# RWKV time mixing: where the value projections run, and where they are kept until the chains use them

## The chip, the cores and the metric

The kernel runs on one core of a Trainium2 chip. The metric is the device time of one execution in microseconds. The program has one launch, on fixed inputs, and is compiled once; a planner in the compiler puts the instructions of each engine in order.

## The reference, cut to what matters

Two layers of an encoder trunk over 256 tokens of width 2048. Each layer is a mixer and a squared-ReLU MLP, both with a norm whose shift, scale and gate come from a conditioning vector. The mixer of the second layer is a bidirectional RWKV-7 with 32 heads of 64:

```python
xr, xw, xk, xv, xa, xg = [h + xx * mu[j] for j in range(6)]
r = heads(xr @ w_r); k = heads(xk @ w_k); v = heads(xv @ w_v)
g = jax.nn.sigmoid(xg @ g1) @ g2
...
sa = jnp.einsum('bhvk,bhk->bhv', state, -kk_t)
state = state * w_t[:, :, None, :] + sa[..., None] * (kk_t * a_t)[:, :, None, :] + v_t[..., None] * k_t[:, :, None, :]
o_t = jnp.einsum('bhvk,bhk->bhv', state, r_t)
...
o = groupnorm(state_out) * gn_g + gn_b
y = ((o + bonus) * g) @ w_o
x = x + gate * y
```

The scan runs once forwards and once backwards. The three projections and the output are products of 256 x 2048 by 2048 x 2048 in float32. The `gate` of the residual is a third of the conditioning's product `silu(c) @ ada_w + ada_b`.

## The kernel before, in words

**Products.** A float32 product is made of three matmuls in a rounded format (lines 510, 511, 512, `prod`): high by high, high by low, low by high. The weights arrive in tiles of 128 x 1024 (512 KB), are cast on ScalarE (line 465) and the rest is taken on VectorE (line 466). A projection is cut in four blocks of 512 columns, one for each four pairs of heads. `stream` (line 999) yields a step for each of 16 row tiles; `rwkv_linear` (line 1025) issues 4 x 3 matmuls of 256 columns in each step. One weight tile and one input tile of 512 KB each serve two steps. `PF` = 3 weight tiles are asked for ahead. They lie in a pool `wp` of six buffers.

**Inputs.** `spill_mixes` (line 1282) makes the token-shifted inputs, split in high and low. The keys' input stays in SBUF (two tiles of 128 x 8 x 2 x 256, `self.xd[2]`); those of the receptances and the values are written to DRAM (`mix0`, `mix3`) and read back once for each block (line 1009).

**The keys stage** (n = 0 to 3). `mains` is a chain of generators: keys and receptances of blocks 0 to 3, then the values of block 0; `in_turn` starts the next one six steps (`LD`) before the last ends. Beside them run two lanes of `rwkv_keys` (line 1339), which make decay, keys and their triangular products for four pairs of heads and write them to DRAM, and `invert` (line 1417), 31 steps of two VectorE operations for a block's triangular inverse. `weave` (line 950) takes a step from the stream that is furthest behind by its weight.

**The chains** (p = 0 to 17). In round p run: the last six steps of chain p - 1 and the first seven of chain p (`pair_chain`, line 1543), with a priority of 1000 (`HA`, `HB`); the preparation of pair p + 1 (`pair_prep`, line 1472; before the rounds that of pair 0); the tail of pair p - 2 (`pair_tail`, line 1622); `MT` steps of `work()`, with `main` as its name; the inverse of block 3 in rounds 0 to 2, then `BG` halves of conditioning in rounds 3 to 14. `pair_load` (line 1445) asks for the data of pair p + 2. `work()` is the values of blocks 1 to 3, and then the output projection `rwkv_out` (line 1052): columns 2 and 3 over eight row tiles, whose sums are put aside in DRAM, then columns 0 and 1, then the rest. A unit of `rwkv_out` waits until the tails have made its row tiles (`ready`, line 1085). Round 17 takes what is left of `main`; after it come the last row tiles and the residual.

**Values.** Those of a block are a tile of 128 x 4 x 256 in SBUF, of pool `vp` or `p2`; `pair_prep` transposes a quarter of it (lines 1487 to 1489), and the tail multiplies it with the bonus (line 1630).

**Conditioning.** `bg` (line 331) keeps `AP` = 5 loads of 512 KB ahead in `wp` and does one half product on VectorE (line 362). 35 halves are left for this layer: 32 for its gate, 3 for the last MLP.

**Order.** The planner goes by priority, which is the order in which the code emits, raised for the chains, and by when inputs are ready. All loads named here are issued by SP, in one queue. `paced` (line 964) ties each step of `main` behind a matmul of the chains. The pools of the keys stage (`ws`, `xt`, `xk`, `rk`, `p1`) are closed before those of the chains (`p2`) open, which take their place in SBUF tile by tile. `pt` (line 944) takes PSUM from two pools of four banks in turn (`PQ`), or from one alone once `npt` is None, which `rwkv_out` sets when it begins.

Of the kernel before, what the change touches and what calls it, by code (L numbers as in the profile page):

```python
# [9 lines left out]
F32 = mybir.dt.float32  # L10
# [22 lines left out]
BG, IV, CH, MT, B0, B1, M0, M1, LD = (10, 10, 10, 10, 10, 10, 10, 10, 10, 5, 5, 5, 5, 5, 5, 5, 5, 5), 12, 7, (5, 5, 5, 5, 5, 5, 5, 5, 5, 5, 5, 2, 3, 2, 3, 2, 3, 2), 3, 14, 6, 6, 6  # L33
PK, PF = 8, 3
# [179 lines left out]
class Build:  # L214
# [21 lines left out]
    def run(self):  # L236
# [4 lines left out]
        self.cut, self.casts, self.wq = None, [], None  # L241
# [222 lines left out]
    def split(self, a, hi, lo, eng=None):  # L464
        c = self.nc.scalar.copy(hi, a)  # L465
        d = (eng or self.nc.vector).tensor_tensor(lo, a, hi, ALU.subtract)  # L466
        if eng is None:
            self.cut = d.ins
            self.casts = [c.ins]
# [18 lines left out]
    def load(self, name, n, i, pools):  # L488

        self.turn += 1  # L490
        w = self.t(pools[self.turn % len(pools)], [P, 2, NB], "w")
        src = self.A[name][n, i // 2][:, i % 2 * 2 : i % 2 * 2 + 2]
        if self.wq is None:
            self.dma = self.nc.sync.dma_start(w, src).ins
        else:
            with self.tc.issue_after(self.casts[-1]):
                self.wq.dma_start(w, src)
        self.tick(self.rate / 2)
        return w
# [499 lines left out]
    def stream(self, name, n, src, tiles):  # L999
# [4 lines left out]
        def ahead(i):  # L1004
            if isinstance(src, list):
                x = src[i // 4][:, 2 * i % 8 : 2 * i % 8 + 2]
            else:
                x = self.t(self.xt, [P, 2, 2, T], "x", bufs=self.xb, dt=F32R)
                nc.sync.dma_start(x.bitcast(F32), src[:, 2 * i : 2 * i + 2])
# [94 lines left out]
    def rwkv(self):  # L1104
# [7 lines left out]
        self.nd = [tc.dram_tile([P, 2, 1024], F32, name=f"nd{b}") for b in range(4)]  # L1112
        self.rx = [tc.dram_tile([4, 32, 1024], F32, name=f"rx{b}") for b in range(4)]
# [3 lines left out]
        with ExitStack() as st:  # L1117
# [5 lines left out]
            vp = self.pool(st, "vp", reuse_waits="tile")  # L1123
            vt = {}

            def values(n, pool):
                def tiles():
                    vt[n] = self.t(pool, [P, 4, T], "v")
                    return vt[n]

                yield from self.rwkv_linear("rw_v", n, 3, tiles)

# [3 lines left out]
            self.xd[2] = [self.t(xk, [P, 8, 2, T], f"xk{i}", dt=F32R) for i in range(2)]  # L1136
# [17 lines left out]
            mains = self.in_turn(mains + [values(0, vp)], LD)  # L1154
            with ExitStack() as st2:
# [12 lines left out]
                self.rate, self.wq = 0.0, None  # L1168
# [6 lines left out]
            with st1:  # L1175
                p1 = self.pool(st1, "p1", reuse_waits="tile")
                for n in range(4):
# [17 lines left out]
                    self.weave((self.take(mains, 34), 34 if n < 3 else 17), (lane(0), 21), (late(), 24), (self.invert(n - 1) if 0 < n <= IB else None, 34))  # L1195
            with ExitStack() as st1:
# [28 lines left out]
                def spread_gate(pool):  # L1225
                    r, g = self.need("tm", 2), self.t(pool, [P, 4, T], "v")
# [7 lines left out]
                self.weave((self.pair_prep(p2, Z[0], vt[0][:, 0, :]), 12), (self.take(main, M1), M1))  # L1234
                chains, self.gates = {}, []
                for p in range(18):
# [3 lines left out]
                    if p < 15:  # L1240
                        nx = self.pair_prep(p2, Z[p + 1], vt[(p + 1) // 4][:, (p + 1) % 4, :])
                    if p == 17:
                        self.npt = None
                        spread_gate(vp)
# [33 lines left out]
        self.wq = None  # L1278
# [3 lines left out]
    def spill_mixes(self, h, xx):  # L1282
        for j in (2, 0, 3):
            for k in range(0, KT, 2):
# [3 lines left out]
                if j == 2:  # L1288
                    x = self.xd[2][k // 8][:, k % 8 : k % 8 + 2]
# [182 lines left out]
    def pair_prep(self, rp, z, v):  # L1472
# [6 lines left out]
        z["v"] = v  # L1479
# [246 lines left out]
```

## Time and profile before

| | |
|---|---|
| runs | 3045.83, 3052.12, 3054.84 us (median 3052.12) |
| profiled execution | 3047.34 us; its span 3045.3 us |
| mean granted clock of TensorE | 0.973 |
| TensorE busy | 2871.4 us, 94% |
| VectorE, ScalarE, GpSimd busy | 2122.1, 1301.6, 522.2 us |
| HBM read, written | 706.08, 42.80 MB |

The span is the time from the first to the last instruction. A stretch is given by its start and end in microseconds from the start of the span. Busy time of TensorE is a union of its matmuls, so work at half clock counts as busy too; beside it stands the clock that was granted, as a share of 2.4 GHz. An "x" stands before a count of instructions. A float32 matmul outside of `prod` is two recorded matmuls. Some records are missing.

### The profile page before, as it was taken

The page shows a single profiled execution, that of the slowest core. Times are in us where ns is not written, and L with a number is a line of the kernel's source. Part 1 is how long each engine was busy: PE and PEld are TensorE (multiplying, and loading weights), DVE is VectorE, ACT ScalarE, POOL GpSimd, SP SyncE. Part 2 cuts the span into 40 slices and gives each one's busy share as a digit, 9 for nine tenths or more (in the row PEclk, how much of TensorE's full clock was granted, in tenths as well). Part 3 has the DMA queues.
Part 4 walks back from the last instruction along what each step waited for, and adds up shares of the span by engine and source line. Part 5 has one row for each costly group of instructions (what it writes and reads, how often), then busy time and mean ns, then how long its engine had stood idle before and what let it go on. Part 6 is the DMA issues. An engine that isn't in the chain of part 4 may idle for free. (4 is left out here: it accounts for less than half of the span.)

```text
span 3045.3 us, 52042 instructions
## 1 busy us (share of the span) xinstructions
PE 2871.4 (94%) x20308; PEld 2488.7 (82%) x20308; DVE 2122.1 (70%) x3126; ACT 1301.6 (43%) x1947; POOL 522.2 (17%) x574
## 2 busy tenths in 40 slices
PE   6999989999999999997999878999998999999998
PEld 2678776789988999886888777777778998899986
DVE  7899866657777788787768875775646776455454
ACT  3233334444443444443466542334445443344443
POOL 1211200011100011004354541322322110001000
PEclk9999999999999999998999987999999999999999
DMA  9978777747898988984987788997545777555552
GB/s 328 326 271 284 243 262 263 247 154 244 287 308 306 304 290 290 313 297 158 323 264 249 266 258 226 301 300 208 149 149 194 245 252 272 193 186 183 202 193 93
DMA packets 279970, 752.30 MB, mean 247 GB/s; under 512 B 73081, under 2 KB 99577, under 8 KB 278572
## 3 DMA queue, kind: packets, MB, share of 16 engines
q1 hardware_dynamic: 279148, 745.38, 73.1%
q8 instruction: 159, 2.61, 0.3%
q10 hardware_dynamic: 576, 3.60, 0.3%
q14 instruction: 87, 0.71, 0.1%
HBM read 706.08 MB, written 42.80 MB: 246 GB/s over the span
## 5 line engine op out<-in xcount | busy, mean ns | idle before, releaser
L466 DVE TENSOR_TENSOR f_wl<-f_w,f_wh 128x1024 fp32r<-128x1024 f32 x512 | 630.8, 1233 | 444.3 <-ACT f_wh L465 433.4
L465 ACT CAST f_wh<-f_w 128x1024 fp32r<-128x1024 f32 x512 | 538.0, 1052 | 748.4 <-PE f_mm L512 315.8
L511 PE MATMUL f_mm<-f_h,f_wh 128*128 128x256 f32 x2048 | 579.5, 283 | 0.0
L510 PE MATMUL f_mm<-f_h,f_wh 128*128 128x256 f32 x2048 | 579.5, 283 | 0.0
L512 PE MATMUL f_mm<-f_h,f_wl 128*128 128x256 f32 x2048 | 579.1, 283 | 0.0
L511 PE MATMUL f_mm<-f_wl,f_hid 128*128 128x512 f32 x1024 | 398.6, 389 | 1.1 <-DVE f_wl L466 1.1
L512 PE MATMUL f_mm<-f_wh,f_hid 128*128 128x512 f32 x1024 | 398.5, 389 | 0.0
L511 PEld LDWEIGHTS f_mm<-f_h,f_wh 128*128 128x128 f32 x2048 | 393.2, 192 | 0.1
L510 PEld LDWEIGHTS f_mm<-f_h,f_wh 128*128 128x128 f32 x2048 | 393.0, 192 | 0.1
L512 PEld LDWEIGHTS f_mm<-f_h,f_wl 128*128 128x128 f32 x2048 | 392.9, 192 | 0.0
L510 PE MATMUL f_mm<-f_wh,f_hid 128*128 128x512 f32 x1024 | 357.9, 389 | 0.0
L362 DVE SCALAR_TENSOR_TENSOR mix_w<-mix_w,mix_s 128x1024 f32<-128x1024 f32 x175 | 219.8, 1265 | 77.0 <-DMA mix_w<-in_ada_f 52.5
L466 POOL TENSOR_TENSOR f_hid<-f_u,f_hid 128x512 fp32r<-128x512 f32 x64 | 98.0, 1531 | 990.6 <-ACT f_hid L465 988.2
L362 DVE SCALAR_TENSOR_TENSOR f_w<-f_w,mix_s 128x1024 f32<-128x1024 f32 x174 | 233.6, 1345 | 2.6 <-DMA f_w<-in_ada_f 2.6
L511 PEld LDWEIGHTS f_mm<-f_wl,f_hid 128*128 128x128 f32 x1024 | 192.2, 188 | 41.3 <-DVE f_wl L466 1.7
L512 PEld LDWEIGHTS f_mm<-f_wh,f_hid 128*128 128x128 f32 x1024 | 192.3, 188 | 39.8
L510 PEld LDWEIGHTS f_mm<-f_wh,f_hid 128*128 128x128 f32 x1024 | 192.2, 188 | 39.7
L466 DVE TENSOR_TENSOR tm_wl<-tm_w,tm_wh 128x1024 fp32r<-128x1024 f32 x128 | 164.4, 1287 | 85.8 <-ACT tm_wh L465 81.6
L465 ACT CAST mix_wh<-mix_w 128x1024 fp32r<-128x1024 f32 x114 | 119.4, 1050 | 201.2 <-PE mix_mm L512 86.3
L510 PE MATMUL tm_mm<-tm_x,tm_wh 128*128 128x256 f32 x512 | 161.2, 316 | 12.3 <-DMA tm_x<-mix 10.8
L465 ACT CAST tm_wh<-tm_w 128x1024 fp32r<-128x1024 f32 x128 | 133.4, 1046 | 86.7 <-PE tm_mm L511 60.3
L466 DVE TENSOR_TENSOR mix_wl<-mix_w,mix_wh 128x1024 fp32r<-128x1024 f32 x114 | 142.4, 1254 | 38.8 <-ACT mix_wh L465 38.7
(456 smaller groups left out, 5494.6 us busy)
## 6 DMA issues: line engine op xcount, KB each, us to landing
f_w<-in_w SPq DMA_DIRECT2D x512, 512.0 KB, 5.1
f_w<-in_ada_f SPq DMA_DIRECT2D x125, 512.0 KB, 5.6
mix_w<-in_ada_mix SPq DMA_DIRECT2D x96, 512.0 KB, 6.2
mix_w<-in_w_in SPq DMA_DIRECT2D x80, 512.0 KB, 5.0
mix_w<-in_ada_f SPq DMA_DIRECT2D x64, 512.0 KB, 5.2
tm_x<-mix SPq DMA_DIRECT2D x64, 512.0 KB, 5.8
f_w<-in_ada_tm SPq DMA_DIRECT2D x49, 512.0 KB, 5.8
mix_w<-in_w_out SPq DMA_DIRECT2D x32, 512.0 KB, 4.6
```

The source lines that it names most:

```text
L362: V.scalar_tensor_tensor(w, w, 1.0, self.s[:, j * (D // 2) : (j + 1) * (D // 2)], ALU.mult, ALU.mult, accum_out=a[:, j, i : i + 1])
L465: c = self.nc.scalar.copy(hi, a)
L466: d = (eng or self.nc.vector).tensor_tensor(lo, a, hi, ALU.subtract)
L510: mm(out, lhsT=l[0], rhs=r[0], start=start, stop=False)
L511: mm(out, lhsT=l[0], rhs=r[1], start=False, stop=False)
L512: mm(out, lhsT=l[1], rhs=r[0], start=False, stop=stop)
```

## The change

The values of all four blocks are projected at the end of `mains`, in the weave of block n = 3 of the keys stage, which now takes 17 x 4 + 1 = 69 steps with a weight of `VL` = 34, where before it took 17 with a weight of 17. When the values' first generator starts, it takes eight tiles in place of the keys' input (which is now eight tiles instead of two) and loads the values' input into them once; all four blocks read it there. The values of a block go to a tile "gate" in `rk` and from there to DRAM (`vd`). `pair_load` reads 128 x 256 of them for each pair, before its other loads, into a tile "v" with six buffers, and `pair_prep` takes them from there. `work()` now begins with the output projection. `MT` is 4 in all rounds (before: 5 in rounds 0 to 10, then 2 and 3 in turn), `BG` is 3 (before: 10 in rounds 0 to 8, then 5). The gate's tile of line 1226 comes from `p2`. The second queue for weights (`wq`, `casts`), which was never set, is gone.

```diff
-BG, IV, CH, MT, ... = (10, 10, 10, 10, 10, 10, 10, 10, 10, 5, 5, ...), 12, 7, (5, 5, 5, 5, 5, 5, 5, 5, 5, 5, 5, 2, 3, 2, 3, 2, 3, 2), ...
+BG, IV, CH, MT, B0, B1, M0, M1, LD = 3, 12, 7, 4, 3, 14, 6, 6, 6
-PK, PF = 8, 3
+PK, PF, VL, NV = 8, 3, 34, 4
...
     def stream(self, name, n, src, tiles):
...
             if isinstance(src, list):
-                x = src[i // 4][:, 2 * i % 8 : 2 * i % 8 + 2]
+                x = src[i]
...
     def rwkv(self):
...
+        self.vd = [tc.dram_tile([P, 4, T], F32, name=f"vd{n}") for n in range(4)]
...
-            vp = self.pool(st, "vp", reuse_waits="tile")
-            vt = {}
-
-            def values(n, pool):
-                def tiles():
-                    vt[n] = self.t(pool, [P, 4, T], "v")
-                    return vt[n]
-
-                yield from self.rwkv_linear("rw_v", n, 3, tiles)
-
...
-            self.xd[2] = [self.t(xk, [P, 8, 2, T], f"xk{i}", dt=F32R) for i in range(2)]
+            resident = lambda: [self.t(xk, [P, 2, 2, T], f"xk{i}", dt=F32R) for i in range(KT // 2)]
+            self.xd[2] = resident()
...
-            mains = self.in_turn(mains + [values(0, vp)], LD)
+
+            def values(n, pool):
+                if n == 0:
+                    self.xd[4] = self.xd[3]
+                    spilt, self.xd[3] = self.xd[3], resident()
+                    for i, x in enumerate(self.xd[3]):
+                        nc.sync.dma_start(x.bitcast(F32), spilt[:, 2 * i : 2 * i + 2])
+                v = []
+
+                def tiles():
+                    v.append(self.t(pool, [P, 4, T], "gate", bufs=1 + (pool is not rk)))
+                    return v[0]
+
+                yield from self.rwkv_linear("rw_v", n, 3 if n < NV else 4, tiles)
+                nc.sync.dma_start(self.vd[n], v[0])
+
+            mains = self.in_turn(mains + [values(n, rk) for n in range(NV)], LD)
...
-                    self.weave((self.take(mains, 34), 34 if n < 3 else 17), (lane(0), 21), (late(), 24), (self.invert(n - 1) if 0 < n <= IB else None, 34))
+                    self.weave((self.take(mains, 34 if n < 3 else 17 * NV + 1), 34 if n < 3 else VL), (lane(0), 21), (late(), 24), (self.invert(n - 1) if 0 < n <= IB else None, 34))
...
                 def work():
-                    for n in range(1, 4):
-                        yield from values(n, (vp, p2)[n % 2])
+                    for n in range(NV, 4):
+                        yield from values(n, p2)
...
-                        nx = self.pair_prep(p2, Z[p + 1], vt[(p + 1) // 4][:, (p + 1) % 4, :])
+                        nx = self.pair_prep(p2, Z[p + 1])
...
     def pair_load(self, rp, p):
...
+        z["v"] = self.t(rp, [P, T], "v", bufs=6)
+        nc.sync.dma_start(z["v"], self.vd[b][:, pb, :])
...
-    def pair_prep(self, rp, z, v):
+    def pair_prep(self, rp, z):
...
-        z["v"] = v
+        v = z["v"]
```

## Rows read from the trace of the kernel before

**Rows 1.** The page, parts 1 and 2 (40 slices of 76.1 us; digits are tenths).

```profile
PE   6999989999999999997999878999998999999998
...
PEclk9999999999999999998999987999999999999999
```

**Rows 2.** Stretch, us; busy (x) of PE, PEld, DVE, ACT, POOL; clock, DMA share, GB/s.

```profile
1743.30:1803.00 59.70, 48.89 (x421) 44.23 (x420) 51.06 (x102) 33.92 (x77) 26.82 (x48) 0.91 0.85 275
1803.00:1890.20 87.20, 71.64 (x648) 61.43 (x648) 45.15 (x101) 21.45 (x46) 16.54 (x33) 0.75 0.81 223
1890.20:2122.90 232.70, 226.10 (x2833) 183.76 (x2832) 162.37 (x347) 96.56 (x240) 65.56 (x104) 0.98 0.88 271
1966.50:1999.80 33.30, 27.22 (x301) 22.37 (x301) 19.91 (x41) 11.16 (x27) 6.25 (x13) 0.85 0.93 286
2122.90:2203.80 80.90, 79.67 (x1118) 61.95 (x1119) 49.72 (x119) 37.52 (x104) 25.53 (x45) 1.00 0.56 157
```

**Rows 3.** Line 510 alone: stretch, us; PE (x), PEld (x); clock, DMA share, GB/s.

```profile
1578.60:1658.60 80.00, 39.46 (x131) 25.48 (x130) 0.96 0.80 266
1743.30:1803.00 59.70, 21.59 (x70) 14.30 (x69) 0.91 0.85 275
1803.00:1890.20 87.20, 20.59 (x59) 13.91 (x58) 0.75 0.81 223
1890.20:2050.60 160.40, 37.57 (x116) 22.30 (x116) 0.97 0.94 293
...
2050.60:2122.90 72.30, 14.05 (x34) 6.42 (x34) 1.00 0.75 222
2122.90:2203.80 80.90, 10.34 (x22) 4.14 (x22) 1.00 0.56 157
2122.90:2234.90 112.00, 16.65 (x36) 6.76 (x36) 1.00 0.49 141
2234.90:2297.50 62.60, 24.38 (x66) 12.16 (x66) 0.99 0.55 183
```

**Rows 4.** Timeline of TensorE in two dense stretches: start us, us, engine, line.

```profile
1803.59 0.28 PE L510 MATMUL tm_mm<-tm_x,tm_wh 128*128 128x256 f32 x1
1803.71 0.28 PE L511 MATMUL tm_mm<-tm_x,tm_wh 128*128 128x256 f32 x1
...
2259.95 0.40 PE L511 MATMUL tm_mm<-tm_wl,tm_xh 128*128 128x512 f32 x1
2260.18 0.39 PE L512 MATMUL tm_mm<-tm_wh,tm_xl 128*128 128x512 f32 x1
```

**Rows 5.** Busy time of two stretches without any projection; columns as in rows 2.

```profile
1865.80:1881.70 15.90, 15.90 (x98) 12.19 (x96) 13.14 (x34) 2.84 (x8) 1.85 (x3) 0.50 0.66 230
1960.60:1978.30 17.70, 16.36 (x242) 12.64 (x240) 14.44 (x33) 7.13 (x21) 6.11 (x10) 1.00 0.93 300
```

**Rows 6.** Timeline of TensorE at two gaps; in brackets the idle time before.

```profile
1855.77 0.58 PE L510 MATMUL tm_mm<-tm_x,tm_wh 128*128 128x256 f32 x1 [4.88 <-DMA tm_x<-mix]
...
1989.72 0.70 PE L1561 MATMUL tm_mm<-tm_Q,tm_M 128*64 128x64 f32 x8 [3.48 <-DVE tm_M L1506]
```

**Rows 7.** Timeline of the SP queue before the first gap.

```profile
1846.82 3.76 SPq L1425 DMA_DIRECT2D tm_E<-nd  x7
1850.62 0.48 SPq L1009 DMA_DIRECT2D tm_x<-mix  x1
```

**Rows 8.** Instructions on the weight tiles: ns least/median/most, first and last start.

```profile
L465 ACT CAST tm_wh<-tm_w x128: 1028/1046/1084, 1381.7 to 2286.6; 128x1024 fp32r<-128x1024 f32 x128
L466 DVE TENSOR_TENSOR tm_wl<-tm_w,tm_wh x128: 1202/1224/2053, 1382.8 to 2288.8; 128x1024 fp32r<-128x1024 f32 x128
L362 DVE SCALAR_TENSOR_TENSOR tm_w<-tm_w,mix_s x35: 1203/1218/2136, 1902.7 to 2048.4; 128x1024 f32<-128x1024 f32 x35
```

**Rows 9.** DMA issues: KB each, median us to landing.

```profile
tm_w<-in_rw_o SPq DMA_DIRECT2D x32, 512.0 KB, 4.6
...
tm_r<-ab SPq DMA_DIRECT2D x32, 128.0 KB, 3.8
```

More of the change, by code (lines that the diff above doesn't have):

```diff
@@ L32 @@
 W1, W2 = 1, 1
-BG, IV, CH, MT, B0, B1, M0, M1, LD = (10, 10, 10, 10, 10, 10, 10, 10, 10, 5, 5, 5, 5, 5, 5, 5, 5, 5), 12, 7, (5, 5, 5, 5, 5, 5, 5, 5, 5, 5, 5, 2, 3, 2, 3, 2, 3, 2), 3, 14, 6, 6, 6
-PK, PF = 8, 3
+BG, IV, CH, MT, B0, B1, M0, M1, LD = 3, 12, 7, 4, 3, 14, 6, 6, 6
+PK, PF, VL, NV = 8, 3, 34, 4
 RH, ZZ = (0, 2.4, 2, 2), 0
@@ L240, in run @@
         self.due, self.rate, self.turn, self.hold, self.starting = 0.0, 0.0, 0, None, False
-        self.cut, self.casts, self.wq = None, [], None
+        self.cut = None
         self.small = self.pool(ctx, "small", bufs=2)
@@ L464, in split @@
     def split(self, a, hi, lo, eng=None):
-        c = self.nc.scalar.copy(hi, a)
+        self.nc.scalar.copy(hi, a)
         d = (eng or self.nc.vector).tensor_tensor(lo, a, hi, ALU.subtract)
@@ L468, in split @@
             self.cut = d.ins
-            self.casts = [c.ins]
     def behind(self):
@@ L491, in load @@
         w = self.t(pools[self.turn % len(pools)], [P, 2, NB], "w")
[L492 to L497, printed above, removed]
+        self.dma = self.nc.sync.dma_start(w, self.A[name][n, i // 2][:, i % 2 * 2 : i % 2 * 2 + 2]).ins
         self.tick(self.rate / 2)
@@ L1167, in rwkv @@
                 self.xstack.close()
-                self.rate, self.wq = 0.0, None
+                self.rate = 0.0
                 mixes = self.spill_mixes(h, xx)
@@ L1225, in spread_gate @@
                 def spread_gate(pool):
-                    r, g = self.need("tm", 2), self.t(pool, [P, 4, T], "v")
+                    r, g = self.need("tm", 2), self.t(pool, [P, 4, T], "gate", bufs=2)
                     for i in range(2):
@@ L1233, in rwkv @@
                     pass
-                self.weave((self.pair_prep(p2, Z[0], vt[0][:, 0, :]), 12), (self.take(main, M1), M1))
+                self.weave((self.pair_prep(p2, Z[0]), 12), (self.take(main, M1), M1))
                 chains, self.gates = {}, []
@@ L1240, in rwkv @@
                     if p < 15:
-                        nx = self.pair_prep(p2, Z[p + 1], vt[(p + 1) // 4][:, (p + 1) % 4, :])
+                        nx = self.pair_prep(p2, Z[p + 1])
                     if p == 17:
                         self.npt = None
-                        spread_gate(vp)
+                        spread_gate(p2)
                     if p < 14:
@@ L1277, in rwkv @@
                     self.residual("tm", n, pts[n])
-        self.wq = None
         self.open_gate()
@@ L1288, in spill_mixes @@
                 if j == 2:
-                    x = self.xd[2][k // 8][:, k % 8 : k % 8 + 2]
+                    x = self.xd[2][k // 2]
                 else:
```

## The prediction

> **What bounds the kernel now.** I read the page first, then the time by stage, then the linear work inside each stage, then the idle time of TensorE and the granted clock, and last the loads. In the page TensorE is busy nearly everywhere, at full clock; past the first slices the place where both dip together is slices 24 and 25 of 40, around 1830 us [rows 1]. That is where the change works. By stage [rows 2, 3]: the last keys stage (values of block 0, inverse of block 2) takes 59.7 us; the chains' start (first preparation, rounds 0 and 1) 87.2 us at a mean clock of 0.75; rounds 2 to 10 232.7 us; rounds 11 to 16 112.0 us; the end 62.6 us. In the rounds from 1890 us on TensorE is busy for 97 to 98% of the time, so what is to be won lies mostly before, and in one round of 33.3 us at 0.85.
>
> A projection's share is told by line 510, which issues one matmul of every three (a "triple") [rows 3]. A dense triple of 256 columns takes 3 x 0.12 = 0.36 us, one of 512 columns (output projection) 3 x 0.23 = 0.69 us [rows 4]. A value projection is 64 triples, 23 us. Of the 256 triples of all four, 70 lie in the keys stage, 59 in the start, 116 in the next six rounds and the last 11 just after.
>
> What a round of chains costs without projections: the four rounds from 2122.9 took 80.9 us with 22 output triples, so (80.9 - 15.2) / 4 = 16.4 us, with (1118 - 66) / 4 = 263 recorded matmuls each, 16.0 per us [rows 2, 3]. Two stretches without any projection stand beside it [rows 5]. One, of 17.7 us, ran 242 matmuls at full clock: 13.7 per us, 19.2 us a round. The other, of 15.9 us, ran 98 at half clock: 6.2 per us, 43 us a round. The two stretches of a low clock hold the longest gaps of TensorE behind 1803: 4.88 us in which it waited for the values' input, and 3.48 us, in the slow round, for a mask product on VectorE [rows 6]. The first of these was made by the SP queue: the load of that input was issued at 1850.62, behind seven loads of the last inverse [rows 7].
>
> **The change, part by part**, each against the profiled run.
>
> Keys stage, block 3: weight 34 against the 34 of the other streams puts 34 instead of 17 steps beside the lanes: 128 triples, not 70. 58 x 0.36 = +20.9 us, to 80.6. The stage of block 1, with 131 triples, took 80.0 [rows 3], so the two agree. VectorE had 51.1 us there and gets seven more differences of 1.22 us [rows 2, 8], 60 us, which is no tighter bound.
>
> Values alone: the other 128 triples run behind the lanes with nothing beside them but what the planner pulls forward. 128 x 0.36 = **+46.1 us**. Per pair of steps TensorE needs 2.9 us, ScalarE's cast 1.05 and VectorE's difference 1.22, so they hide; the inverse of block 3, whose loads queued at 1846, can use VectorE here.
>
> Start of the chains: 87.2 us with 59 triples and 648 - 177 = 471 chain matmuls. The triples go, the input and value weights go from the queue, but the fill goes too. Bounds: all at 13.7 per us, 34.4 us; all at 6.2, 76 us. I take the first preparation (122 matmuls of the code) at 16.0 per us, as its loads can come while the values run: 7.6 us. The other 349 I put halfway between the two rates, 25.5 and 56.3: 40.9 us, because the nearest row is this very stretch, whose clock was 0.75, halfway between 1.2 and 2.4 GHz. 48.5 against 87.2: **-38.7 us**.
>
> The clock is where a page speaks. The row shows 15.90 us of 15.9 busy at 0.50 throughout [rows 5]: busy alone did not bring the clock back. The Trainium skill (TensorE: Matmul & The Clock Gate, Part 1) says that the throttled state is the default and that sustained activity releases it. By that sentence alone a start without gaps would run at full clock, and the sum would have 34.4 us here, 14 better than taken; the trace disagrees in this stretch, and the sum goes by the trace.
>
> Rounds 2 to 10: 232.7 us. The triples in it cost 116 x 0.36 + 11 x 0.36 + 23 x 0.69 = 61.6 us, leaving 19.0 a round, the slow round included. Afterwards only the output projection fills. Its steps wait for tails: columns 2 and 3 of the output go forward by 2, 0, 4, 0, 4, 0, 4 steps in rounds 4 to 10 (each pair of row tiles needs two more tails, and a unit starts only when the next one's input is ready). 14 steps are 28 triples, 19.3 us. The rounds themselves lie between 16.4 (well filled) and 19.2 (unfilled); nearer to the latter, 18.5. 9 x 18.5 + 19.3 = 185.8: **-46.9 us** (bounds -66 and -41).
>
> Rounds 11 to 16: four steps each, 48 triples for 36, 12 x 0.69 = +8.3. The end: the output has 128 triples, so 52 are left instead of 66: -9.7.
>
> Loads. The eight resident tiles, 4.2 MB, are asked for six steps before the last receptance projection ends, ahead of its last input. At the 266 GB/s of a keys stage that is 16 us [rows 3], against six steps of 80/34 = 2.4 us. Some of it shows: +3 (0 to +8). They replace 32 loads of 512 KB, 24 of them in the chains. The sixteen reads and four writes of the values through DRAM are hidden: a 128 KB read lands in 3.8 us [rows 9] and is issued two rounds ahead; bare it would be that once, at the first pair.
>
> Gate conditioning: 35 halves of 1.22 us on VectorE, now all between 1902.7 and 2048.4 [rows 8], become 3 a round over rounds 3 to 14. Nothing is added: VectorE has 49.7 us of 80.9 in the late rounds [rows 2]. But the five loads held ahead keep five of six weight buffers, so output weights come one at a time: a landing of 4.6 us [rows 9] and 2.3 of splitting for 2.8 of matmuls. Two units a round fit in 20 us, so 0; at worst +10, if steps slide to the end. PSUM: the output's generator now starts at once and confines the chains to four banks from the first round; the late rounds ran so at 16.4, so 0.
>
> Sum: 20.9 + 46.1 - 38.7 - 46.9 + 8.3 - 9.7 + 3 = **-17 us**. The profiled execution took 3047.3 us (span 3045.3); that gives 3030. The median shown, 3052.1, is 4.8 above it: **3035 us**.
>
> **The rivals.** *The clock stays down (slower).* Place: from the first preparation to round 3, where no projection is left to run. It needs a gap such as those of [rows 6], after which the chain work alone does not lift the clock, as in the 15.9 us. Price: the start at 76 us, +27.5, so +10 in all; if rounds 2 and 3 run so as well, 2 x (43 - 18.5) = 49 more. In the middle, +35: 3087. It decides once the whole start runs at half clock. For it: a one-chain start has less to put between its waits. Against: the 17.7 us that stayed at full clock.
>
> *Nothing gained.* The start repeats what it lost: 87.2 - 21.2 = 66 us, and the sum is 0: 3052. The change may also not do what it says: the planner, which orders instructions by priority and readiness and gives the chains 1000 more, may leave values among the chains after all, and little moves. For: the clock of 0.75 stood there although 59 triples ran. Against: the queue that made the longest gap [rows 7] loses its values.
>
> *The start runs at full clock.* The loads of the first pairs land while the values still run, the chains' work follows without a gap, and the clock stays up: 34.4 us, and rounds at 17.5, so -14 - 9 on top, 3012. For: the 17.7 us at 13.7 per us. Against: the first pairs' tiles take the place of tiles that the values use to the end. It is also what the sentence of the Trainium skill (TensorE: Matmul & The Clock Gate, Part 1) would give.
>
> **How the numbers follow.** The forecast has 0.44 with its own range 3022 to 3046; the clock staying down 0.26, nothing 0.17, the full clock 0.13. The range 3010 to 3087 takes in the full clock and the clock's middle price, and leaves its worst (3111) out. 0.3% (9 us) is about what a measurement of this kernel can tell from no change. Faster: 0.13 + 0.39 of the forecast = 0.52; slower: the clock's and a little of the rest, 0.28; the rest 0.20.
>
> **What would show it.** Right: values' copies ending some 125 us after 1743; about 46 us of triples at 0.12 us spacing; 45 to 52 us to the first chain's output copy with a clock near 0.75; rounds of 18 to 19 us, none of 33; conditioning spread to round 14. Wrong: a start over 66 us or rounds 2 and 3 over 25 us at a clock of 0.5; a keys stage over 90 us, with VectorE as the one waited for; long waits for output weights behind conditioning loads.

## The result, and the profile after

The changed kernel takes 3076.2 us (3073.3 to 3079.0, 4 runs) beside 3053.5 us for the kernel before (4 runs): ratio 1.0086, 95% interval 1.0068 to 1.0104, 23 us by the medians. The forecast was 3035 us, faster; the time lies inside the range, on the wrong side. The profiled execution has a span of 3072.9 us, 27.6 over that of before. What stands ahead of 1743 us is the same within a microsecond, so the stretch from there to the last MLP carries it.

The page after, part 2 (40 slices of 76.8 us), answers to [rows 1]:

```profile
PE   5998989999999999997998996899998999999998
...
PEclk9999999999999999999999996689999999999999
```

TensorE's dip is now in slice 25 (6 tenths), and the clock has 6, 6 and 8 tenths in slices 25 to 27, where it had 8 and 7 in slices 24 and 25. Time by stage after: stretch, us; busy (x) of PE, PEld, DVE, ACT, POOL; clock, DMA share, GB/s. In order: the last keys stage, values alone, start of the chains to the first output copy, rounds 2 to 10, rounds 11 to 16, the end.

```profile
1743.90:1816.50 72.60, 66.58 (x586) 62.56 (x584) 61.90 (x111) 43.73 (x88) 32.36 (x54) 0.98 0.74 222
1816.50:1862.10 45.60, 45.32 (x373) 44.70 (x371) 28.52 (x51) 15.71 (x19) 0.00 (x0) 1.00 0.83 246
1862.10:1947.70 85.60, 51.92 (x490) 42.32 (x490) 43.55 (x97) 17.54 (x39) 13.29 (x27) 0.52 0.81 240
1947.70:2149.80 202.10, 182.90 (x2450) 146.46 (x2451) 114.90 (x276) 79.06 (x223) 58.37 (x106) 0.86 0.66 184
2149.80:2273.90 124.10, 121.67 (x1500) 94.28 (x1500) 72.55 (x167) 57.49 (x145) 35.46 (x56) 0.97 0.54 159
2273.90:2326.90 53.00, 41.36 (x178) 30.86 (x178) 32.00 (x46) 23.36 (x42) 13.17 (x10) 0.93 0.54 174
```

Against [rows 2] the two projection stages and the end are as forecast or better. The start is not: 85.6 us at a clock of 0.52, against 87.2 us at 0.75 before, with the 59 projection triples gone. The same stretches with line 504 alone (the first matmul of a triple, line 510 before), against [rows 3], show that the values did move:

```profile
1743.90:1816.50 72.60, 38.09 (x126) 24.24 (x125) 0.98 0.74 222
1816.50:1862.10 45.60, 34.97 (x124) 23.61 (x123) 1.00 0.83 246
1862.10:1947.70 85.60, 0.00 (x0) 0.00 (x0) 0.52 0.81 240
1947.70:2149.80 202.10, 16.24 (x31) 7.01 (x31) 0.86 0.66 184
```

The start opens with a pause. TensorE's own waits there (line waited at, releaser: us, times, longest):

```profile
PE tm_ps L1490 <- DMA tm_v<-vd: 22.1, 1, 22.1
```

SP's queue at that time (start us, length of the group, count) shows why: the first pair's values are asked for at 1881.32, behind output weights, conditioning blocks (line 327; six of them in the group at 1855.94) and the loads of later steps.

```profile
1855.94 11.23 SPq L327 DMA_DIRECT2D tm_w<-in_ada_tm  x6
...
1872.84 2.60 SPq L1555 DMA_DIRECT2D tm_r<-ab  x4
...
1881.32 0.38 SPq L1451 DMA_DIRECT2D tm_v<-vd  x1
```

And VectorE, from the start to round 10, stands for conditioning blocks that have not landed (before, in rounds 2 to 10, it did so for 13.1 us, 8 times):

```profile
DVE tm_w L362 <- DMA tm_w<-in_ada_tm: 40.9, 17, 6.9
```

So there were three suspects: the pause and SP's order, the missing fill with its low clock, and the conditioning.

### The profile page after: what moved, and what is told of

It is laid out like the page before. It is cut to its first block, busy times and chain, and to the rows that moved or that the text cites. A ratio compares the mean times of both kernels' runs of the same rounds, so it can differ in the third digit from the quotient of the medians.

```text
span 3072.9 us, 52029 instructions
## 1 busy us (share of the span) xinstructions
PE 2861.8 (93%) x20308; PEld 2488.4 (81%) x20308; DVE 2116.1 (69%) x3126; ACT 1304.7 (42%) x1947; POOL 515.3 (17%) x574
## 5 line engine op out<-in xcount | busy, mean ns | idle before, releaser
L505 PEld LDWEIGHTS f_mm<-f_wl,f_hid 128*128 128x128 f32 x1024 | 192.2, 188 | 40.9 <-DVE f_wl L466 1.3
L465 ACT CAST mix_wh<-mix_w 128x1024 fp32r<-128x1024 f32 x114 | 119.5, 1050 | 202.2 <-PE mix_mm L506 85.7
L505 PE MATMUL tm_mm<-tm_xk,tm_wh 128*128 128x256 f32 x512 | 147.9, 290 | 6.1 <-POOL tm_xk L466 6.1
```

What stands on the lines that cost most here:

```text
L505: mm(out, lhsT=l[0], rhs=r[1], start=False, stop=False)
```

## The experiments

Times are medians; a ratio stands against the kernel before on the same chip, with its 95% interval. The kernel before took 3045.8 to 3050.0 us beside these runs. The theories in the expectations are lettered through the whole series.

### The pause, and the clock

**Pair 0's loads first in SP's queue.** Output weights, conditioning blocks and three later loads of the chains (tm_r, tm_bon, tm_g) are tied behind the last load that `pair_load` makes for pair 0. One load of pair 0 is not among those moved forward: tm_a, which `pair_prep` asks for.

```diff
+    def tied(self):
+        return self.tc.issue_after(self.tie) if self.tie is not None else nullcontext()
...
+        with self.tied():
+            self.dma = self.nc.sync.dma_start(w, ...).ins
...
+        if p == 0:
+            self.tie = last.ins
```

> The changed kernel with one thing altered: pair 0's loads (its values, keys and inverse) are put ahead of every output weight, every conditioning load and the chains' later loads in SP's queue. Theory A (the 22.1 us without any matmul after the last value projection come from the order of SP's queue, and that pause brings the clock down): the pause shrinks to 3 to 8 us, the start of the chains (1862.1 to 1947.7, 85.6 us, granted clock 0.52) falls to 48 to 60 us at a clock over 0.8, and the kernel takes 3035 to 3052 us. Theory B (chain work without projection fill is slow and pulls the clock down by itself): the pause goes, but the start stays at a clock of 0.5 to 0.6 and is 68 us or more; 3056 to 3065 us. Theory C (the loads wait for memory, not for their place in the queue): pause and time stay as they are, 3070 to 3080 us.

3078.8 us, 1.0106 (1.0089 to 1.0123): no gain. Start and rounds 2 to 10:

```profile
1864.80:1939.80 75.00, 51.35 (x490) 41.59 (x490) 28.10 (x62) 17.36 (x39) 15.54 (x29) 0.52 0.81 247
1939.80:2154.40 214.60, 187.63 (x2451) 148.48 (x2451) 125.79 (x298) 78.60 (x221) 61.37 (x104) 0.86 0.69 202
```

TensorE's two longest waits there, and the issue of pair 0's tm_a in SP's queue:

```profile
PE tm_ps L1573 <- POOL tm_M L1519: 9.5, 1, 9.5
PE tm_ps L1498 <- DMA tm_v<-vd: 5.9, 2, 4.5
```

```profile
1888.54 1.23 SPq L1495 DMA_DIRECT2D tm_a<-ab  x2
```

The pause fell to 4.5 us and the start by 10.6, but the clock stayed at 0.52, and rounds 2 to 10 took 12.5 us more. Theory A's numbers fall: a pause a fifth as long left the clock as low. That the pause brings the clock down does not fall with them, for the clock fell inside the 4.5 us that were left: it is 1.00 up to 1867.4 us, and TensorE had stopped at 1864.1. A second pause of 9.5 us follows in the first round, where TensorE waits for a copy on GpSimd (tm_M) whose input is tm_a, asked for behind the loads of pair 1. B has the clock right and the total wrong, as the start's gain was given back in the rounds behind it.

**Matmuls that nobody reads in the pause.**

```diff
+                with tc.issue_after(self.lastmm):
+                    for _ in range(26):
+                        self.warm = nc.tensor.matmul(dummy, lhsT=self.ident, rhs=self.s[:, :NB], start=True, stop=True).ins
...
+        with self.tc.issue_after(self.warm) if z["p"] == 0 else nullcontext():
+            PE.transpose(vp[:, 1, :], v[:, :P], self.ident)
```

> The changed kernel with 26 matmuls that nobody reads (128x512, fp32, into a bank of their own) between the last value projection and pair 0's first transpose; the pair's loads keep their place in SP's queue. Separates the clock from the pause. Theory A: the clock is still full when the pair's loads land, so the start of the chains is some 22 us of these matmuls and 45 to 50 us of chain work, 65 to 73 us in all, and the kernel takes 3050 to 3064 us. Theory B: the clock falls as soon as the chains are alone, whatever came before; the start stays at 80 us or more and the kernel at 3070 to 3082 us.

3091.1 us, 1.0142 (1.0127 to 1.0157), worse than either theory had it; of the 15 us above the changed kernel 10 lie in rounds 2 to 10 (212.2 us), for a reason that the run doesn't show. The stretch of the extra matmuls, then the chains alone, in three parts:

```profile
1864.50:1886.90 22.40, 22.40 (x57) 9.94 (x55) 19.57 (x48) 3.31 (x4) 2.58 (x7) 1.00 0.93 280
1886.90:1893.80 6.90, 5.41 (x77) 4.26 (x76) 4.45 (x9) 3.52 (x4) 0.74 (x2) 1.00 0.54 124
1893.80:1902.50 8.70, 0.01 (x1) 0.00 (x0) 0.00 (x0) 0.00 (x0) 0.93 (x3) 0.62 0.64 182
1902.50:1948.50 46.00, 42.49 (x409) 34.90 (x409) 16.04 (x37) 10.55 (x32) 8.26 (x18) 0.50 0.76 225
```

The middle part is a pause, and what ended it is the same copy on GpSimd as above:

```profile
PE tm_ps L1570 <- POOL tm_M L1517: 8.7, 1, 8.7
```

The clock entered the chains at 1.00, was at 1.00 in their first 6.9 us, fell in a pause of 8.7 us, and then stayed at 0.50 through 46 us in which TensorE was busy for 42.5. So the start holds more than one wait for a late load, and here the clock fell in the second when the first was filled; the chains' work did not lift it again in those 46 us. That is not quite theory B, by which it falls as soon as the chains are alone. It can fall with a short pause only, too: in round 2 of the changed kernel it does so at 1950.6 us, with none over 0.6 us just before. The Trainium skill (TensorE: Matmul & The Clock Gate, Part 1) says that sustained activity releases the throttle. Here, as in [rows 5], a TensorE that was nearly always busy, with small float32 matmuls, stayed throttled all the same, and the trace decides.

### How many values ahead

**Two of four ahead**, two among the chains as fill.

```diff
-PK, PF, VL, NV = 8, 3, 34, 4
+PK, PF, VL, NV = 8, 3, 34, 2
...
-                self.open_linear(st1, 2, W2, 3)
+                self.open_linear(st1, 2, W2, 2)
```

> The changed kernel with two of the four value projections ahead of the chains, and two woven into the chains as fill (their input is streamed from DRAM, two buffers deep; all values still go through DRAM). The values' stretch alone halves (45.6 to about 23 us). Theory A: what the two cost beside the chains is hidden in part, but the pause of 22 us and the low clock after it stay unless the queue's order happens to change: 3060 to 3080 us. Theory B (fill is what is missing): the start runs at a clock over 0.7 and rounds 2 to 10 near the 202 us of the changed kernel or below: 3035 to 3058 us.

**One ahead**, three among the chains, with the main work per round of before.

```diff
-PK, PF, VL, NV = 8, 3, 34, 4
+PK, PF, VL, NV = 8, 3, 17, 1
...
-BG, IV, CH, MT, B0, B1, M0, M1, LD = 3, 12, 7, 4, 3, 14, 6, 6, 6
+BG, IV, CH, MT, B0, B1, M0, M1, LD = 3, 12, 7, (5, 5, 5, 5, 5, 5, 5, 5, 5, 5, 5, 2, 3, 2, 3, 2, 3, 2), 3, 14, 6, 6, 6
```

(with the shallower input buffer, as above)

> The changed kernel with one value projection ahead of the chains, three among them, and the main work per round (5 steps, then 2 and 3) of the kernel before; what stays of the change is that the values go through DRAM, the input's tiles are split in eight, and the conditioning's rate. Theories A and B (where the values run, and what it does to the start, is the whole difference): 3045 to 3062 us, with the start near the 87 us of the kernel before. Theory D (the way through DRAM or the conditioning's rate costs something by itself): 3066 us or more.

Two ahead: 3063.8 us, 1.0059 (1.0042 to 1.0077). One ahead: 3070.2 us, 1.0086 (1.0069 to 1.0103), as slow as the change itself with the values placed nearly as before. That is theory D. (Two ahead has a time in theory A's range, but the clock of theory B in its start, 0.78.) So where the values run is not what made the kernel slower. What all these kernels share is the way through DRAM, the input's tiles in eight parts and the conditioning's rate.

### The conditioning's rate

The four edits are one: `BG` is 3 in the kernel before, or the tuple 10 (rounds 3 to 8), 5 (9 to 14) in the others.

```diff
-BG, ... = 3, ...
+BG, ... = (10, 10, 10, 10, 10, 10, 10, 10, 10, 5, 5, 5, 5, 5, 5, 5, 5, 5), ...
```

> The kernel BEFORE with the conditioning's rate of the change alone (3 units in every round instead of 10 and then 5); nothing else. Theory D (the rate itself costs time, since 35 halves of 1.2 us on VectorE move out of rounds 2 to 8, where the value projections keep TensorE supplied, into later rounds that VectorE's steps bound): 3056 to 3072 us. Theory E (the conditioning is off the path wherever it stands): 3042 to 3052 us.

> The one-ahead kernel (values 0 ahead of the chains, 1 to 3 among them, all kept in DRAM, the streamed input two buffers deep) with the conditioning's rate of the kernel before. What is left of the change is the way through DRAM with its smaller memory. Theory D: 3045 to 3058 us, as the kernel before. Theory E with the cost in the DRAM path or in the shallower input buffer: 3065 to 3080 us, as the one-ahead kernel.

> The changed kernel with the conditioning's rate of the kernel before; all four value projections stay ahead of the chains. Theory D: the changed kernel falls by 8 to 20 us, to 3055 to 3068. Theory E: 3070 to 3082 us. If theory B holds (the chains alone bring the clock down), the first round still ends 70 us or more after the last value projection in either case.

> The two-ahead kernel with the conditioning's rate of the kernel before. Theory D with theory B (fill keeps the clock of the chains up, and the rate is a cost of its own): 3040 to 3055 us, the best of the series, rounds of 26 us falling to 23 to 25. Theory E: 3058 to 3070 us, as the two-ahead kernel.

| values ahead | 10, then 5 | 3 a round | none in the chains (below) |
|---|---|---|---|
| before (one, kept in SBUF) | 1 | 1.0044 (1.0025 to 1.0063) | 0.9954 (0.9937 to 0.9971) |
| one, through DRAM | 1.0010 (0.9995 to 1.0025) | 1.0086 (1.0069 to 1.0103) | |
| two | 0.9988 (0.9974 to 1.0003) | 1.0059 (1.0042 to 1.0077) | |
| all four | 1.0019 (1.0005 to 1.0032) | 1.0086 (1.0068 to 1.0104) | 0.9934 (0.9909 to 0.9958) |

Theory D holds in every line: the rate costs 0.4 to 0.8%, in the changed kernel more than the 8 to 20 us that were expected. The first column says the rest: with the rate of before, moving the values and the way through DRAM come out between 0.1% faster and 0.2% slower. In the second column, at a rate of 3, one ahead and all four ahead are both 0.4% slower than the kernel that keeps its values in SBUF (two ahead 0.15%, within noise). So the rate and the way through DRAM, with what came along with it, cost more together; why is not shown. In microseconds the changed kernel falls from 3076.2 to 3052.1 with the old rate alone, beside 3049.3 for the kernel before.

Start, rounds 2 to 10 and 11 to 16 of the changed kernel with the old rate:

```profile
1859.70:1941.40 81.70, 49.31 (x490) 40.28 (x490) 45.18 (x103) 17.53 (x40) 14.90 (x27) 0.56 0.85 268
1941.40:2132.50 191.10, 175.65 (x2475) 139.38 (x2477) 116.04 (x281) 78.19 (x222) 60.42 (x105) 0.93 0.71 204
2132.50:2252.00 119.50, 118.69 (x1479) 92.31 (x1480) 67.82 (x160) 57.85 (x145) 36.73 (x56) 1.00 0.51 150
```

VectorE's wait for blocks over start and rounds 2 to 10:

```profile
DVE tm_w L362 <- DMA tm_w<-in_ada_tm: 16.8, 7, 8.6
```

Its halves in this layer (ns least/median/most, first and last start):

```profile
L362 DVE SCALAR_TENSOR_TENSOR tm_w<-tm_w,mix_s x35: 1206/1224/1229, 1847.2 to 1989.1; 128x1024 f32<-128x1024 f32 x35
```

Of the 22 us between the two traces (stages 583.0 and 561.0 us) 11.0 lie in rounds 2 to 10, 4.6 in rounds 11 to 16, 3.9 in the start, 2.2 in the end. VectorE's waits for blocks fell from 40.9 us to 16.8. The last of the 35 halves starts at 1989 us; at a rate of 3, by the same view of the changed kernel, at 2318.

### What in the conditioning costs

**No blocks loaded** (left out: this stage's conditioning data), VectorE's halves kept.

```diff
-                w = self.t(self.wp, [P, D // 2], "w")
+                w = self.t(self.wp, [P, D // 2], "w") if s != "tm" else None
...
+        b = w if w is not None else self.s[:, : D // 2]
+        w = w if w is not None else self.t(self.wp, [P, D // 2], "w")
```

> The changed kernel with the conditioning's blocks not loaded in this layer's stage: its 35 halves multiply a vector that is always there and write to a weight buffer taken at that moment (left out: the conditioning's data of this stage, so the result of the layer's gate is not the reference's). VectorE's work and its places stay. In the changed kernel VectorE stands 28.4 us of rounds 2 to 10 before 11 halves until their block lands; with the rate of before it stood 6.4 us. Theory F (a half whose block is late blocks VectorE's queue, and the chains behind it): 3045 to 3060 us. Theory G (it is the 1.2 us of VectorE's own time in each round): 3066 to 3080 us.

3027.8 us, 0.9940 (0.9922 to 0.9958): 48 us below the changed kernel (45 by the ratios) with VectorE's work all there. Theory G falls, and the loads cost more than theory F had. (The 28.4 us of waiting that the expectation gives to rounds 2 to 10 are of rounds 2 to 16; rounds 2 to 10 have 25.9.) Start and rounds 2 to 10:

```profile
1860.10:1928.30 68.20, 53.34 (x490) 43.30 (x490) 39.50 (x93) 17.41 (x40) 13.82 (x29) 0.52 0.78 231
1928.30:2104.20 175.90, 166.51 (x2483) 133.06 (x2483) 111.59 (x265) 78.35 (x222) 60.10 (x103) 0.97 0.60 163
```

**Blocks loaded, VectorE's multiplication left out.**

```diff
+        if self.label == "tm":
+            V.memset(a[:, j, i : i + 1], 0.0)
+        else:
             V.scalar_tensor_tensor(w, w, 1.0, self.s[...], ALU.mult, ALU.mult, accum_out=...)
```

> The changed kernel with the opposite left out: the conditioning's blocks are loaded as before, and VectorE's multiplication of each half is left out in this stage (a one-column fill stands for it; the layer's gate is not the reference's). Theories F and G both say the rate's cost goes with it: 3040 to 3058 us. Theory H (the loads themselves, their 35 places in SP's queue and their hold on the six weight buffers, are the cost): 3064 to 3080 us.

3063.8 us, 1.0058 (1.0038 to 1.0079): only 12 us off, outside the range of theories F and G and at the edge of H's. SP's waits from the start to round 10:

```profile
SPq L327 <- DMA tm_w<-in_ada_tm: 25.9, 13, 6.1
SPq L494 <- DMA tm_w<-in_ada_tm: 15.5, 8, 3.3
```

With no half to wait, SP itself stands 41.4 us, in the middle of its queue, until an earlier block has landed in the buffer that the next conditioning block (line 327) or output weight (line 494) is to take. In the changed kernel SP stands at its line 327 too, but there until VectorE has freed a buffer:

```profile
SPq L327 <- DVE tm_w L362: 12.1, 5, 4.3
```

So the two queues hold each other up, and without the halves SP alone stands.

**An eighth of the bytes** (64 KB a block; left out: the rest of the data).

```diff
-                self.nc.sync.dma_start(w, self.A["ada_" + u[0]][u[1] * KT + i][:, j])
+                    self.nc.sync.dma_start(w[:, :P], self.A["ada_" + u[0]][u[1] * KT + i][:, j, :P])
...
```

> The changed kernel with the conditioning's loads of this layer's stage cut to an eighth of their bytes (64 KB each instead of 512), in the same places of SP's queue, into the same buffers, with a VectorE half of 7/8 of its length on what is there (left out: the rest of the blocks, so the layer's gate is not the reference's). Without the loads the kernel took 3028 us. Theory J (the bytes: the transfers share the DMA engines with the pairs' loads, DMA share 0.81 in the start): 3026 to 3042 us. Theory K (the places in SP's queue and the six shared buffers, whatever the bytes): 3058 to 3078 us.

**One block ahead instead of five.**

```diff
-            while len(self.ada_next) < AP:
+            while len(self.ada_next) < (1 if self.label == "tm" else AP):
```

> The changed kernel with one conditioning block loaded ahead of its use in this stage instead of five; all is computed. Theory L (five blocks held in the six shared weight buffers keep the output weights out): 3045 to 3062 us. If it is the wait of VectorE for a block that lands late, a shorter lead makes it longer: 3078 to 3100 us. Theory J (bytes): 3070 to 3080 us, unchanged.

3070.4 us, 1.0063 (1.0039 to 1.0087), and 3072.2 us, 1.0063 (1.0041 to 1.0085). The bytes and the five buffers held are a small part of the cost at most, 6 and 4 us of the 48, and neither is clear of noise. VectorE's waits, in the one and in the other:

```profile
DVE tm_w L370 <- DMA tm_w<-in_ada_tm: 29.6, 16, 7.2
```

```profile
DVE tm_w L362 <- DMA tm_w<-in_ada_tm: 32.2, 17, 6.3
```

Blocks of 64 KB were still waited for 29.6 us, against 40.9 for blocks of 512. They are late because they are asked for late, in SP's one queue: in the changed kernel, for instance, the block that VectorE waits for until 1960.2 us was issued at 1956.7 and landed 3.5 us later. That is theory K, reached mostly by leaving out the others: no run keeps these loads and takes them out of SP's queue. How much of the 48 us is VectorE's wait and how much SP's the runs don't settle, because the planner makes a new order for each kernel.

**The kernel before without the blocks** (left out: the same data).

> The kernel BEFORE with this stage's conditioning blocks not loaded (its halves multiply a vector that is always there; left out: the conditioning's data of this stage, so the layer's gate is not the reference's). The changed kernel without them took 3028 us. If moving the values is worth by itself what the forecast's sum gave it (17 us): 3042 to 3048 us here, since the kernel before hides its conditioning beside the value projections. If the move is worth nothing by itself: 3023 to 3034 us.

3054.4 us, 1.0017 (1.0005 to 1.0030): no gain, and outside both ranges. Taken by itself this would say that the kernel before hides its conditioning. But VectorE's halves, which have nothing to wait for now, crowd into rounds 2 to 4, 27 of them instead of 17:

```profile
L365 DVE SCALAR_TENSOR_TENSOR tm_w<-mix_s 128x1024 f32<-128x1024 f32 x27 | 33.0, 1231 | 0.2
```

Those three rounds took 94.7 us (1890.1 to 1984.8) instead of 76.3. So VectorE's own time is not free where it is crowded, and the run is no clean removal; the section on the conditioning out of the chains has one.

### The old rate, with order and fill

**Loads first, old rate**, and then **28 matmuls that nobody reads woven into the start and the first two rounds**:

```diff
+                    for i in range(20):
+                        dummy = self.t(self.mm, [P, NB], "mm") if i >= 6 else None
+                        for _ in range(2 if i >= 6 else 0):
+                            with self.paced():
+                                nc.tensor.matmul(dummy, lhsT=self.ident, rhs=self.s[:, :NB], start=True, stop=True)
+                        yield 1
```

> The changed kernel with the conditioning's rate of the kernel before, and pair 0's loads ahead of the weights in SP's queue as in the first run of the series. At the changed rate that order gained 10 us at the start and lost it again. If the loss came from the conditioning (theories F, G or H), the gain now stays: 3038 to 3048 us, against 3052 without the order. If the order only moves the wait (output weights late in the first rounds): 3050 to 3058 us.

> The kernel of the run above with 28 matmuls that nobody reads (128x512, fp32), two at a time, woven into the first pair's preparation and the first two rounds, where nothing is left to fill them. Theory B (the chains alone don't hold TensorE's clock, and the low clock is what the start costs): the granted clock of the start rises from 0.56 to over 0.85, the start falls by 15 to 30 us against the run above, and the kernel takes 3018 to 3035 us, below both. If the start is bound by the chain's steps between the engines, and not by TensorE's clock: the same as the run above within 5 us, or up to 24 us slower (28 times 0.86 us).

3069.5 us, 1.0075 (1.0053 to 1.0096), and 3063.7 us, 1.0057 (1.0039 to 1.0074). The first is above both of its ranges; the second misses theory B's, and lies 5.8 us below the run without fill. Another order of SP's queue alone, with the same loads, cost 17 us (3052.1 to 3069.5). The order moves the conditioning back: its first half starts at 1922.4 us here, at 1847.2 without the order (row above), and rounds 2 to 10 take 211.1 us instead of 191.1. Start and rounds 2 to 10 without and with the extra matmuls:

```profile
1868.20:1942.50 74.30, 44.11 (x490) 35.86 (x490) 30.01 (x67) 16.46 (x38) 16.16 (x29) 0.63 0.81 251
1942.50:2153.60 211.10, 187.59 (x2475) 148.01 (x2477) 131.78 (x309) 79.43 (x222) 59.18 (x102) 0.86 0.74 222
```

```profile
1867.70:1944.20 76.50, 63.82 (x570) 40.50 (x569) 26.73 (x60) 16.54 (x39) 15.26 (x28) 0.80 0.84 267
1944.20:2145.60 201.40, 186.93 (x2449) 146.98 (x2450) 135.41 (x311) 79.67 (x222) 61.85 (x104) 0.90 0.75 223
```

The extra matmuls alone, in the start:

```profile
1867.70:1944.20 76.50, 26.60 (x48) 9.69 (x47) 0.80 0.84 267
```

The fill lifted the clock of the start from 0.63 to 0.80, and the start did not get shorter; the rounds behind it were 9.7 us shorter. But the fill itself kept TensorE busy for 26.6 us of the start, so what the clock gave back and what the fill took can cancel. What the low clock by itself costs the start is not shown.

### The conditioning out of the chains

**In the feed-forward stage ahead**, nothing left out.

```diff
-RHY, RGL, RWO, RF0, RF1 = 2.4, 2, 0.6, 1.2, 0.8
+RHY, RGL, RWO, RF0, RF1 = 2.4, 2, 0.6, 1.5, 0.8
...
-BG, IV, CH, MT, B0, B1, M0, M1, LD = 3, 12, 7, 4, 3, 14, 6, 6, 6
+BG, IV, CH, MT, B0, B1, M0, M1, LD = 1, 12, 7, 4, 3, 14, 6, 6, 6
...
-            todo += [(q, i) for q in SUBS for i in range(2)]
+            todo += [(q, i) for q in SUBS for i in range(2)] + [("tm", 2)]
```

> The changed kernel with the time mixing's gate conditioning (32 halves) done in the feed-forward stage ahead of it, at a rate of 1.5 instead of 1.2 units for two weight loads, and none left among the chains; nothing is left out. If the feed-forward stage has room for it (VectorE and the DMA engines not bound there): 3026 to 3036 us, faster than both kernels. If it has not: the stage ahead grows by what the layer's stage saves (32 halves of 1.2 us of VectorE, or 16.8 MB of transfers), 3050 to 3075 us.

3033.3 us, 0.9934 (0.9909 to 0.9958), faster than both kernels. In the trace all 35 halves run in the stage ahead, the three of the last MLP too. The stages in the order of the first table:

```profile
1740.40:1813.10 72.70, 67.25 (x582) 63.53 (x581) 60.42 (x111) 42.85 (x85) 30.80 (x54) 0.95 0.72 218
1813.10:1859.20 46.10, 45.47 (x376) 45.16 (x375) 33.66 (x66) 16.50 (x19) 0.52 (x2) 1.00 0.74 226
1859.20:1924.60 65.40, 47.92 (x490) 39.17 (x490) 21.67 (x52) 17.47 (x39) 12.68 (x30) 0.58 0.80 233
1924.60:2109.30 184.70, 169.31 (x2475) 133.85 (x2475) 98.43 (x243) 78.65 (x221) 54.17 (x102) 0.96 0.58 154
2109.30:2228.70 119.40, 118.78 (x1480) 92.33 (x1480) 67.72 (x160) 57.84 (x146) 36.66 (x56) 1.00 0.52 151
2228.70:2279.60 50.90, 40.95 (x177) 30.52 (x176) 29.02 (x45) 25.42 (x44) 13.17 (x10) 0.95 0.50 163
```

The stage that took the work over paid nothing: 730.2 us here, 730.3 in the changed kernel, VectorE going from 560.0 to 594.6 us busy beside a TensorE that is busy throughout.

```profile
645.50:1375.70 730.20, 730.14 (x4704) 669.75 (x4704) 594.62 (x767) 314.10 (x349) 57.85 (x40) 1.00 0.88 310
```

**The same on the kernel before**, and **the same on the changed kernel with pair 0's loads first**:

> The kernel BEFORE with the gate conditioning done in the feed-forward stage ahead at a rate of 1.5, nothing left out. If the kernel before hides its conditioning beside the value projections (as the run without its loads says): 3046 to 3058 us, and the values' move is worth 13 to 25 us by itself. If it too pays for it: 3025 to 3038 us, and the move is worth nothing.

> The changed kernel with the conditioning in the feed-forward stage (3033 us), and pair 0's loads put ahead of the output weights and of the chains' later loads in SP's queue. With the conditioning among the chains this order made things worse by 3 us at the change's rate and by 17 at the rate of before. If that was because it pushed conditioning blocks back: the pause of 10.3 us without a matmul shrinks to about 5, nothing is lost later, 3024 to 3032 us. If output weights and later loads are lost by it all the same: 3036 to 3050 us.

The kernel before so treated takes 3033.6 us, 0.9954 (0.9937 to 0.9971): it pays for its conditioning too, 13 us, against 43 in the changed kernel. Its stages (keys, start, rounds 2 to 10, 11 to 16, end) sum to 544.4 us, the changed kernel's above to 539.2; in the medians nothing is left of the difference.

```profile
1744.70:1804.00 59.30, 48.06 (x417) 43.48 (x416) 50.31 (x102) 33.09 (x75) 27.03 (x48) 0.91 0.87 272
1804.00:1894.30 90.30, 71.67 (x652) 61.13 (x651) 44.92 (x102) 21.91 (x47) 17.38 (x33) 0.74 0.80 216
1894.30:2112.00 217.70, 217.70 (x2830) 178.37 (x2831) 118.47 (x264) 96.47 (x240) 59.17 (x104) 1.00 0.70 205
2112.00:2223.80 111.80, 109.66 (x1454) 84.22 (x1452) 65.42 (x157) 52.34 (x140) 34.56 (x55) 1.00 0.49 141
2223.80:2289.10 65.30, 55.52 (x239) 41.94 (x238) 36.08 (x50) 32.17 (x53) 17.09 (x13) 0.98 0.58 193
```

With pair 0's loads first: 3028.4 us, 0.9940 (0.9917 to 0.9963), the same as without. The wait for the values halved (10.3 us to 4.8), yet the start took 71.7 us and rounds 2 to 10 175.9. TensorE waited 7.7 us for the copy of tm_a here, which was again asked for behind the loads of pair 1. These three kernels can't be told apart; each is 13 to 18 us faster than the kernel before.

## Why the prediction was wrong

- **Keys stage and values alone, 80.6, 46.1 and +3 for the resident loads:** 72.6 and 45.6, with 126 and 124 triples. The count was right, and the loads did not show. In the keys stage the new triples did not all come on top: TensorE was idle there for 10.8 us before and for 6.0 after. Together 11.5 us better than forecast.
- **Start of the chains, 48.5: the failed step.** 85.6 us, +37.1. Two parts of the term failed. The first preparation was to run at full rate in 7.6 us, "as its loads can come while the values run", and the reads of the values through DRAM were to be hidden. They came late, behind output weights, conditioning blocks and later loads in SP's queue, and TensorE stood 22.1 us. The rest, 63.5 us, was 490 recorded matmuls at 7.7 per us and a clock of 0.50, not halfway between the two rates of [rows 5]: another 15 us. That half was taken from this very stretch, whose clock of 0.75 had been granted with 59 triples in it, and these moved out. With no conditioning in the chains the start is 65.4 us, 10.3 of them pause, so about 17 us of the miss belong to this term and 20 to the conditioning's.
- **Rounds 2 to 10, 185.8:** 202.1. With the conditioning elsewhere 184.7, so the sum of this term was right for chains and output, and the miss of 16 us is conditioning. But the 232.7 us that it started from had conditioning in them as well: without it the kernel before takes 217.7. So 15 us of the 46.9 that were to be won here were the price of conditioning, read as time of the rounds. **Rounds 11 to 16** (120.3) took 124.1, and 119.4 to 119.5 with the rate of before or none; **the end** (52.9) 53.0.
- **Gate conditioning, 0, at worst +10: the second failed step.** The rate alone costs 20 to 24 us in the changed kernel (1.0086 against 1.0019; 3076 against 3052) and 11 to 13 in the kernel before. The working counted VectorE's time and the buffers. Neither is the main cost: halves without loads, three a round, cost nothing that shows, and a lookahead of one changed little. What was left out is the two in-order queues: each block has a place in SP's queue, in which pair loads and output weights stand behind it, and each half a place in VectorE's, in which the chain's steps stand behind a block that is late. The Trainium skill (Perfetto Trace Analysis, Per-engine timelines) calls VectorE's queue strictly first in, first out; the 40.9 us of waiting at line 362 agree. The prediction did name "long waits for output weights behind conditioning loads" as a sign of being wrong, without a price.
- **The conditioning of the kernel before** was taken as free too, though VectorE waits 13.1 us for its blocks there. Taken out of the chains, it gives 13 us.
- **The rival "the clock stays down"** priced the start at 76 us; it took 85.6, or 63.5 without its gap. Rounds 2 and 3 took 30.7 and 15.9 us from output copy to output copy, far below its 43 each. Its mechanism is what the trace has: a gap, of 22.1 us, in which the clock fell, and chain work that did not lift it again until 1947 us. Its price left out the gap itself and had the rate too slow. Whether the low clock is what made the start slow is open, since the one run that raised it paid with fill.
- **The move itself,** -17 in the sum, gains nothing that is clear of noise. Against the kernel before at the same rate, the kernel with all four ahead is 0.4% slower at a rate of 3, 0.2% slower at the old one, and not told apart with the conditioning away. In the last case the stages say how: 59.5 us more in keys and values, against 24.9 less in the start, 33.0 less in rounds 2 to 10, 7.6 more in rounds 11 to 16 and 14.4 less at the end. The projections' time is nearly the same anywhere; what the sum hoped to win beside it was the slow start, and a start without fill stays slow.

What stays open: what the start would take with all of pair 0's loads in time, tm_a too, and the clock up (no run has both; without conditioning blocks the runs took 65 to 72 us), the share of SP's and of VectorE's waits in the conditioning's cost, and why the way through DRAM costs more at a rate of 3.

## What to carry to other kernels

Price background work by its places in the in-order queues, its loads' too, and not by its busy time: ask what stands behind a block that lands late. Put it where one engine is bound and dense for long (here a feed-forward stage that took 35 more halves for nothing). When a stage is taken as the base of a sum, ask what else it pays for. When a change bundles a move with new constants, cost and try the constants by themselves first: here one constant put back takes the loss from 0.86% to 0.19%.

## What the runs showed that was not expected

- After a pause of 8.7 us the granted clock stayed at 0.50 through 46 us in which TensorE was busy for 42.5 us with chain matmuls.
- Blocks of 64 KB were waited for 29.6 us in 16 waits, blocks of 512 KB 40.9 us in 17, and the kernel's time hardly changed: an eighth of the bytes took away a quarter of the waiting.
- Raising the start's clock from 0.63 to 0.80 with 26.6 us of fill left it at 74 to 77 us.
- With pair 0's loads "first", one of them still came late: the copy of tm_a on GpSimd held TensorE for 9.5 us.
